# Low half of k stored in both halves of the partitions: the second score product on 128 rows

## The chip, the cores and the metric

The kernel runs on one NeuronCore of a Trainium2 chip. The metric is the device time of one execution in microseconds (us); less is better. PE is the matrix engine, PEld its weight loads, DVE, ACT and POOL the vector, scalar and GpSimd engines, SP the engine whose queue issues most DMAs.

## The reference

One decoder layer in float32 on 1024 tokens of width 1024: LayerNorm, a projection, two attention groups side by side, an output projection, LayerNorm, a SwiGLU feed-forward block (width 2816), LayerNorm. The scores of both groups are what the change touches:

```python
# stick-breaking group: 8 heads of 64, causal
z = einsum('bhqd,bkhd->bhqk', q_blk, k) * Dh ** -0.5
log_1m_beta = where(causal, log_sigmoid(-z), 0.0)
suffix = cumsum(log_1m_beta, reverse=True) - log_1m_beta
attn = where(causal, exp(log_sigmoid(z) + suffix), 0.0)
out = einsum('bhqk,bkhd->bqhd', attn, v)
# sliding-window group: 8 query heads over 2 k/v heads, window 128
logits = einsum('bnqhgd,bnchd->bnhgqc', qb, kb) * Dh ** -0.5
p = softmax(where(valid, logits + bias, -inf), with a sink logit per head)
```

## The kernel before, in words

Every float32 operand of a product is split into a high part (rounded to float32r) and a low part (the rest), and a product of two operands is made of three matrix products, high by high, high by low and low by high (`mm3`, lines 114 to 120). In the scores a head has only 64 dimensions, so the split is laid along the 128 partitions instead. The tile `q` of a head holds the high part of q on 64 partitions and the low part on the other 64 (`put_q`, L279 and L280). The tile `kd[e]` of head e holds the high part of k twice, on both halves (`put_k`, ACT, L272 and L273), so one product over 128 rows gives (q high + q low) by k high. The low part of k stands once, in one tile `kl` for two heads, head e on its own 64 partitions (`put_k`, DVE, L274). The second product of the scores reads only these 64 rows:

```python
pe.matmul(ps, qs[:, tok], kd[:, keys], start=True, stop=False)
pe.matmul(ps, qs[r, tok], kl[r, keys], start=False, stop=True)
```

These are L384 and L385 in the stick-breaking group (`sb_unit`, output `z`) and L318 and L319 in the sliding-window group (`swa_attend`, output `lg`). There are 96 and 64 such pairs.

The program runs in stages. First entry LayerNorm, with k, v and q of the first sliding-window group and its attention (to about 132 us). Then the attention of the second sliding-window group beside the projection of the first pair of stick-breaking heads (132 to 208 us). Then, for pairs 0 to 2, the attention of a pair beside the projection of the next (208 to 412 us). Then the attention of pair 3 beside the first half of the output projection (`c1_steps`, 412 to 510 us). Then the second half of the output projection and the feed-forward block, in which none of this occurs. `merge` traces two such streams side by side; a scheduler then sets the order of the instructions on every engine.

Weights come as strips of 512 KB over SP (`w_raw`, L136) into two `raw` buffers, are split by ACT (L72) and POOL (L73), and are read by the projection `pp` (L120). The tiles q, kd, kl and v, the loads `m` and `res` of the output projection, and some others share one pool of 17 buffers of 4 KB a partition (`U`, tag `u`). A pair of heads takes seven of them: two q, two kd, one kl, two v. `out_load` (L456) fetches `m`, `wo_fill` fetches `w_out` through `raw`, both over SP. SP takes its DMAs in order; one that waits holds up those behind it.

Of the kernel before, what the change touches and what calls it, by code (L numbers as in the profile page):

```python
# [16 lines left out]
ALU = mybir.AluOpType  # L17
# [4 lines left out]
P = 128  # L22
S = 1024
# [22 lines left out]
def _f(ap):  # L46
    return ap.bitcast(F32)
# [3 lines left out]
def layer(ctx: ExitStack, tc: tile.TileContext, x, ln_in, w_sw, w_sb, norm_g,  # L51
# [68 lines left out]
                pe.matmul(ps, a, b, start=(i == 0), stop=(i == n - 1))  # L120
                i += 1

    # the tokens' chunks 2 and 3 make room for the residual, 0 and 1 for half of w_out
    rp = ctx.enter_context(tc.tile_pool(name="rp", bufs=4, side="right", reuse_waits="tile"))
    c1 = ExitStack()
    c1p = c1.enter_context(tc.tile_pool(name="c1p", bufs=4, side="right", reuse_waits="tile"))
# [34 lines left out]
            yield v  # L161

    def merge(a, ta, b, tb):
        # two streams traced side by side in step with their shares; the first goes ahead
        a = ahead(a)
        ca = cb = 0.0
        while a is not None or b is not None:
            if b is None or (a is not None and ca / ta <= cb / tb):
                v = next(a, None)
                if v is None:  # L170
                    a = None
                else:
                    ca += v
            else:
                v = next(b, None)
                if v is None:
                    b = None
                else:
                    cb += v
# [7 lines left out]
    def U(shape, name, dt=F32R):  # L187
        return ub.tile(shape, dt, tag="u", name=name)
# [1 line left out]
    def attile(shape, name, dt=F32R):  # L190
        return bb.tile(shape, dt, tag="at", bufs=AB, name=name)

    # ---- entry LayerNorm
    xts = {}

    def load_x(t):
# [1 line left out]
        for h in ((slice(0, 512), slice(512, D)) if t == 0 else (slice(0, D),)):  # L198
            sp.dma_start(xts[t][:, h], x[t * P:(t + 1) * P, h])

    # the bias reaches all partitions over a product with a row of ones
    row = U([1, D], "row", F32)
    sp.dma_start(row, ln_in[1].unsqueeze(0))
    load_x(0)
# [61 lines left out]
        return ps.rearrange("p a b -> p (a b)"), slice(c0 * 256, (c0 + nc_) * 256)  # L266

    def put_k(ps, tok, kd, kl):
        # the high halves stand twice, so that one product meets both halves of q
        for e in range(2):  # L270
            a, b = slice(e * 64, e * 64 + 64), slice(64 - e * 64, 128 - e * 64)
            act.copy(kd[e][a, tok], ps[a])  # L272
            act.copy(kd[e][b, tok], ps[a])  # L273
            dve.tensor_tensor(out=kl[a, tok], in0=ps[a], in1=_f(kd[e][a, tok]), op=ALU.subtract)  # L274

    def put_q(ps, tok, q, e, hi_row):
        r = slice(e * 64, e * 64 + 64)
# [2 lines left out]
        dve.tensor_tensor(out=q[l, tok], in0=ps[r], in1=_f(q[h, tok]), op=ALU.subtract)  # L280

    def put_v(ps, c0, nc_, vts):
        # vts[e][:, t] holds [high | low] of head e for token tile t
        n = 2 * nc_
        vr = ws.tile([P, n, P], F32, tag="raw", bufs=2, name="vr")
        dve.tensor_copy(vr.rearrange("p a b -> p (a b)"), ps)
        pv = bps.tile([P, n, 2, 64], F32, tag="pp", name="pv")
        for i in range(n):
            pe.transpose(pv[:, i], vr[:, i, :], ident)
        for e in range(2):  # L290
            split_ps(pv[:, :, e, :], vts[e][:, 2 * c0:2 * c0 + n, 0, :], vts[e][:, 2 * c0:2 * c0 + n, 1, :])

    # ---- sliding-window group
    def swa_q(g, i, q, c0, nc_):
        ps, tok = xmul(strip(2 + 2 * g + i), c0, nc_)
        for e in range(2):
# [6 lines left out]
                yield 1.0  # L303

    def swa_attend(g, q, kd, kl, vts, bias):
        h = slice(g * 64, g * 64 + 64)
        for n in range(NT):
            tok = slice(n * P, (n + 1) * P)
            nk = P if n == 0 else 2 * P
            kb = nk // P  # L310
            keys = slice((n + 1) * P - nk, (n + 1) * P)
            Ls = []
            nm = st.tile([P, 4], F32, tag="nm", name="nm")
            for i in range(2):
                ps = bps.tile([P, 2, nk], F32, tag="z", bufs=ZB, name="lg")
                for e in range(2):
                    j = 2 * i + e
                    pe.matmul(ps[:, e, :], q[j][:, tok], kd[g][:, keys], start=True, stop=False)  # L318
                    pe.matmul(ps[:, e, :], q[j][h, tok], kl[h, keys], start=False, stop=True)  # L319
                L = bb.tile([P, 2, nk], F32, tag=("s1", "s2")[i], bufs=SB, name="L")  # L320
                dve.scalar_tensor_tensor(out=L, in0=ps, scalar=SCALE,
                                         in1=bias[:, 2 * i:2 * i + 2, 0:nk][:, :, ::-1],
                                         op0=ALU.mult, op1=ALU.add)
                dve.tensor_reduce(out=nm[:, 2 * i:2 * i + 2], in_=L, axis=AX.X, op=ALU.max, negate=True)
                Ls.append(L)
            hs = slice(4 * g, 4 * g + 4)
            dve.tensor_tensor(out=nm, in0=nm, in1=nsink[:, hs], op=ALU.min)
            es = st.tile([P, 4], F32, tag="es", name="es")
            dve.tensor_tensor(out=es, in0=sink[:, hs], in1=nm, op=ALU.add)
            den = st.tile([P, 4], F32, tag="den", name="den")  # L330
            for j in range(4):
                act.activation(Ls[j // 2][:, j % 2, :], Ls[j // 2][:, j % 2, :], AF.Exp, bias=nm[:, j:j + 1],
                               accum_out=den[:, j:j + 1])
            act.activation(es, es, AF.Exp)
            dve.tensor_tensor(out=den, in0=den, in1=es, op=ALU.add)
            rd = st.tile([P, 4], F32, tag="rd", name="rd")
            dve.reciprocal(rd, den)
            for i in range(2):
                pool.tensor_tensor(out=Ls[i], in0=Ls[i],
                                   in1=rd[:, 2 * i:2 * i + 2].unsqueeze(2).broadcast_to([P, 2, nk]), op=ALU.mult)  # L340
            av = bps.tile([P, 4, P], F32, tag="av", name="av")
            for b in range(kb):
                at = attile([P, 2, 4, P], "at")
                ah, al = at[:, 0], at[:, 1]
                ps = bps.tile([P, 4, P], F32, tag="tr", name="trp")
                for j in range(4):
                    pe.transpose(ps[:, j, :], Ls[j // 2][:, j % 2, b * P:(b + 1) * P], ident)
                split_ps(ps, ah, al)
                v = vts[g][:, n - kb + 1 + b].rearrange("p a d -> p (a d)")
                pe.matmul(av, v, ah, start=(b == 0), stop=False)  # L350
                pe.matmul(av, v, al, start=False, stop=(b == kb - 1))
            oT = bb.tile([P, 2, P], F32, tag="oT", name="oT")
            for e in range(2):
                r = slice(e * 64, e * 64 + 64)
                act.copy(oT[r], av[64:128, e::2, :])
                dve.tensor_tensor(out=oT[r], in0=av[0:64, e::2, :], in1=oT[r], op=ALU.add)
            for i in range(2):
                act.dma_start(o_dram[4 + 2 * g + i][:, tok], oT[:, i, :])
            yield 1.0

    # ---- stick-breaking group, two heads at a time
    def sb_project(p, qs, kd, kl, vts):
        for w in range(3):
            for c in range(2):
# [8 lines left out]
                yield 1.0  # L373

    def sb_unit(qs, kd, kl, e, qb, t0, t1, carry):
        # weights of the keys of tiles t0..t1 for one query block, walked from the right
        w = (t1 - t0) * P
        keys = slice(t0 * P, t1 * P)
        tok = slice(qb * P, (qb + 1) * P)
        s1 = bb.tile([P, w], F32, tag="s1", bufs=SB, name="s1")  # L380
        s2 = bb.tile([P, w + 1], F32, tag="s2", bufs=SB, name="s2")
        r = slice(e * 64, e * 64 + 64)
        ps = bps.tile([P, w], F32, tag="z", bufs=ZB, name="z")
        pe.matmul(ps, qs[:, tok], kd[:, keys], start=True, stop=False)  # L384
        pe.matmul(ps, qs[r, tok], kl[r, keys], start=False, stop=True)  # L385
        act.activation(s2[:, 0:w], ps, AF.Sigmoid, scale=-SCALE)
        act.activation(s1, ps, AF.Sigmoid, scale=SCALE)
        last = t1 - 1 == qb
        if last:
            # keys at or after the query neither take weight nor break the stick  # L390
            pool.affine_select(out=s1[:, w - P:], in_=s1[:, w - P:], pattern=[[-1, P]], base=0,
                               channel_multiplier=1, compare_op=ALU.is_gt, fill=0.0)
        else:
            pool.tensor_copy(s2[:, w:w + 1], carry)
# [10 lines left out]
    def sb_attend(p, qs, kd, kl, vts):  # L405
        for c in range(4):
            oT = bb.tile([P, 256], F32, tag="oT", name="oT")
            for e in range(2):
# [3 lines left out]
                for t0, t1 in ([(0, nb)] if nb <= 4 else [(4, nb), (0, 4)]):  # L412
                    ats = [attile([P, 2, 2, 2, P], "at") for u in range(t0, t1, 2)]
                    for i in range(2):
                        qb = 2 * c + i
                        te = min(t1, qb + 1)
                        A, carry[i] = sb_unit(qs[e], kd[e], kl, e, qb, t0, te, carry[i])
                        m = te - t0
                        ps = bps.tile([P, m, P], F32, tag="tr", name="tra")
                        for j in range(m):  # L420
# [19 lines left out]
                            act.dma_start(o_dram[p][:, c * 256:(c + 1) * 256], oT)  # L440
                    yield float(m)

    # ---- output projection
    def wo_fill(k, hi, lo):
        raw = w_raw(w_out[k * P:(k + 1) * P, :], (P, D))
        act.activation(hi, raw, AF.Copy, scale=gT[:, k:k + 1])
# [37 lines left out]
    def units():  # L484
        bias0 = load_bias(0)
        q0 = [U([P, S], "q") for _ in range(4)]
        kd = [U([P, S], "kd") for _ in range(2)]
        kl = U([P, S], "kl")
        vts = [U([P, NT, 2, 64], "v") for _ in range(2)]
        return bias0, q0, kd, kl, vts  # L490

# [26 lines left out]
    merge(att0, 2, swa_project(1, q1), 4)  # L518

    def sb_tiles():  # L520
        return ([U([P, S], "q") for _ in range(2)], [U([P, S], "kd") for _ in range(2)], U([P, S], "kl"),
                [U([P, NT, 2, 64], "v") for _ in range(2)])

    cur = sb_tiles()
# [54 lines left out]
                    pe.transpose(ps[:, i, :], acc[t][:, k * P:(k + 1) * P], ident)  # L579
                split_ps(ps, hh[cc][:, 4 * g:4 * g + 4, o:o + P], hl[cc][:, 4 * g:4 * g + 4, o:o + P])  # L580

    # ---- FFN and last post-LayerNorm
    fq = [(f, j) for f in range(NF) for j in range(2)]
    fl = []

# [137 lines left out]
```

## Time and profile before

| what | value |
|---|---|
| three runs | 1319.35, 1320.6, 1322.6 us, median 1320.6 |
| profiled execution, first to last instruction | 1319.7 us |
| what lies around it | no own time is listed for the profiled execution; its span stands 0.9 us under the median of the runs |
| PE busy | 1273.9 us (97%) |
| PEld, DVE, POOL, ACT busy | 1051.3, 644.3, 484.7, 472.2 us |
| mean granted PE clock | 0.987 of full speed |

Matrix products are pipelined: the next one starts before the one before it has ended. So what a product takes of PE's time is read from the start of one row of the timeline to the start of the next, not from its duration.

### The profile page before, as it was taken

Reading aid. Unit: us, or ns where it says so; the run is one execution under the profiler, and the core shown is the slowest. Engines: PE = TensorE matmul, PEld = TensorE weight load, DVE = VectorE, ACT = ScalarE, POOL = GpSimd, SP = SyncE. Lnnn points to the kernel's source line nnn. Section 1 sums busy time; section 2 is a strip of 40 time slices with the busy share of each in tenths; the row PEclk is TensorE's granted clock in tenths of the full one; section 3 lists DMA queues with packets and bytes.
Section 4 is the critical chain, followed back from the end, with each engine's and each line's share of the span. In section 5 each row is a group of like instructions: output and inputs, shape, how many; then the busy total and the mean of one; then the engine's idle time right before and its main releaser. Section 6 shows DMA issues by size and latency. Waiting matters only on the chain. (4 is left out here: it accounts for less than half of the span.)

```text
span 1319.7 us, 17018 instructions
## 1 busy us (share of the span) xinstructions
PE 1273.9 (97%) x6606; PEld 1051.3 (80%) x6606; DVE 644.3 (49%) x1028; ACT 472.2 (36%) x986; POOL 484.7 (37%) x452
## 2 busy tenths in 40 slices
PE   5799999999999999999999999999999999999997
PEld 3688988888887777878888888888888888888886
DVE  8875676787778887862242222221222123212248
ACT  4565566766667654442032002200221022102111
POOL 5413333555545856763042004210321032103224
PEclk9899999999999899999999999999999999999999
DMA  7212102010104411112122102200221022102112
GB/s 268 85 40 73 33 13 60 17 53 13 54 20 137 135 56 59 46 65 80 32 80 64 32 16 80 65 32 16 67 77 32 16 64 80 32 16 64 33 51 109
DMA packets 31919, 78.25 MB, mean 59 GB/s; under 512 B 3764, under 2 KB 15069, under 8 KB 31838
## 3 DMA queue, kind: packets, MB, share of 16 engines
q1 hardware_dynamic: 23614, 68.49, 16.3%
q10 hardware_dynamic: 8224, 8.67, 1.9%
q8 instruction: 52, 0.85, 0.3%
q14 instruction: 29, 0.24, 0.1%
HBM read 64.55 MB, written 12.60 MB: 58 GB/s over the span
## 5 line engine op out<-in xcount | busy, mean ns | idle before, releaser
L73 POOL TENSOR_TENSOR wlo<-raw,whi 128x1024 fp32r<-128x1024 f32 x61 | 146.3, 2400 | 390.2 <-ACT whi L72 387.0
L120 PE MATMUL pgu<-hl,whi 128*128 128x512 f32 x704 | 277.5, 394 | 0.0
L120 PE MATMUL pgu<-hh,wlo 128*128 128x512 f32 x704 | 277.5, 395 | 0.0
L120 PE MATMUL pgu<-hh,whi 128*128 128x512 f32 x704 | 277.3, 394 | 0.0
L627 DVE SCALAR_TENSOR_TENSOR acc<-acc,pd 128x512 f32<-128x512 f32 (+1 forms) x97 | 65.9, 681 | 215.2 <-PE pd L120 215.2
L120 PE MATMUL pp<-xh,whi 128*128 128x256 f32 x544 | 160.1, 295 | 0.4 <-DVE q L280 0.4
L120 PE MATMUL pp<-xh,wlo 128*128 128x256 f32 x544 | 157.7, 290 | 0.0
L609 DVE TENSOR_TENSOR sg<-sg,pgu 128x512 f32<-128x512 f32 x44 | 30.2, 687 | 261.2 <-PE pgu L120 260.8
L120 PEld LDWEIGHTS pgu<-hh,wlo 128*128 128x128 f32 x704 | 131.8, 187 | 32.2
L120 PEld LDWEIGHTS pgu<-hl,whi 128*128 128x128 f32 x704 | 131.8, 187 | 32.1
L120 PEld LDWEIGHTS pgu<-hh,whi 128*128 128x128 f32 x704 | 131.7, 187 | 32.2 <-ACT sg L606 0.2
L120 PE MATMUL pp<-xl,whi 128*128 128x256 f32 x544 | 156.8, 288 | 0.0
L72 ACT CAST whi<-raw 128x1024 fp32r<-128x1024 f32 x61 | 64.1, 1051 | 258.4 <-PE pgu L120 204.7
L120 PE MATMUL pd<-wdl,ah 128*128 128x512 f32 (+1 forms) x356 | 138.1, 388 | 0.0
L120 PE MATMUL pd<-wdh,ah 128*128 128x512 f32 (+1 forms) x356 | 137.8, 387 | 0.0
L120 PE MATMUL pd<-wdh,al 128*128 128x512 f32 (+1 forms) x356 | 137.7, 387 | 0.0
L120 PEld LDWEIGHTS pp<-xh,whi 128*128 128x128 f32 x544 | 105.1, 193 | 5.1 <-issue 2.3
L120 PEld LDWEIGHTS pp<-xh,wlo 128*128 128x128 f32 x544 | 104.6, 192 | 4.3 <-issue 2.9
L120 PEld LDWEIGHTS pp<-xl,whi 128*128 128x128 f32 x544 | 105.1, 193 | 3.6 <-issue 2.4
L73 POOL TENSOR_TENSOR wdl<-raw,wdh 128x1024 fp32r<-128x1024 f32 x22 | 54.8, 2495 | 135.8 <-ACT wdh L72 135.8
L399 POOL TENSOR_TENSOR s<-s,s 128x127 f32<-128x127 f32 (+2 forms) x96 | 86.6, 905 | 45.8 <-DVE s L395 20.7
L612 DVE TENSOR_TENSOR al<-sg,ah 128x512 fp32r<-128x512 f32 x44 | 78.3, 1781 | 46.9 <-ACT ah L611 46.9
(146 smaller groups left out, 2178.6 us busy)
## 6 DMA issues: line engine op xcount, KB each, us to landing
raw<-in_w_gu SPq DMA_DIRECT2D x44, 512.0 KB, 3.6
raw<-in_w_down SPq DMA_DIRECT2D x22, 512.0 KB, 3.6
raw<-in_w_sb SPq DMA_DIRECT2D x12, 512.0 KB, 3.7
h_dram<-x ACTq DMA_DIRECT2D x8, 512.0 KB, 2.9
m<-o_dram SPq DMA_DIRECT2D x32, 128.0 KB, 2.5
res<-h_dram SPq DMA_DIRECT2D x8, 512.0 KB, 3.9
raw<-in_w_out SPq DMA_DIRECT2D x8, 512.0 KB, 4.2
x<-in_x SPq DMA_DIRECT2D x7, 512.0 KB, 6.8
```

What stands on the lines that cost most here:

```text
L72: act.copy(hi, raw)
L73: pool.tensor_tensor(out=lo, in0=raw, in1=_f(hi), op=ALU.subtract)
L120: pe.matmul(ps, a, b, start=(i == 0), stop=(i == n - 1))
L399: pool.tensor_tensor(out=s1[:, 0:m], in0=s1[:, 0:m], in1=s2[:, 1:m + 1], op=ALU.mult)
L609: dve.tensor_tensor(out=sg, in0=sg, in1=ps, op=ALU.mult)
L612: dve.tensor_tensor(out=al[:, tok], in0=sg, in1=_f(ah[:, tok]), op=ALU.subtract)
L627: dve.scalar_tensor_tensor(out=acc[t][:, ds], in0=acc[t][:, ds], scalar=(ALPHA if ci == 0 else 1.0), in1=pd, op0=ALU.mult, op1=ALU.add)
```

## The change

`kl` becomes a list of two tiles, one a head, as `kd` is. DVE writes the low part of k on the head's own 64 partitions as before, and a DMA on SP's queue copies it to the other 64 partitions of the same tile. Both second products then read all 128 rows: q high and q low, each by k low. The low by low term, which the kernel before left out, is so added to the scores. A pair takes eight buffers of the pool of 17.

```diff
 def put_k(ps, tok, kd, kl):
     for e in range(2):
         a, b = slice(e * 64, e * 64 + 64), slice(64 - e * 64, 128 - e * 64)
         act.copy(kd[e][a, tok], ps[a])
         act.copy(kd[e][b, tok], ps[a])
-        dve.tensor_tensor(out=kl[a, tok], in0=ps[a], in1=_f(kd[e][a, tok]), op=ALU.subtract)
+        dve.tensor_tensor(out=kl[e][a, tok], in0=ps[a], in1=_f(kd[e][a, tok]), op=ALU.subtract)
+        sp.dma_start(_f(kl[e][b, tok]), _f(kl[e][a, tok]))
...
 def swa_attend(g, q, kd, kl, vts, bias):
-    h = slice(g * 64, g * 64 + 64)
...
                 pe.matmul(ps[:, e, :], q[j][:, tok], kd[g][:, keys], start=True, stop=False)
-                pe.matmul(ps[:, e, :], q[j][h, tok], kl[h, keys], start=False, stop=True)
+                pe.matmul(ps[:, e, :], q[j][:, tok], kl[g][:, keys], start=False, stop=True)
...
 def sb_unit(qs, kd, kl, e, qb, t0, t1, carry):
-    r = slice(e * 64, e * 64 + 64)
     pe.matmul(ps, qs[:, tok], kd[:, keys], start=True, stop=False)
-    pe.matmul(ps, qs[r, tok], kl[r, keys], start=False, stop=True)
+    pe.matmul(ps, qs[:, tok], kl[:, keys], start=False, stop=True)
...
-                        A, carry[i] = sb_unit(qs[e], kd[e], kl, e, qb, t0, te, carry[i])
+                        A, carry[i] = sb_unit(qs[e], kd[e], kl[e], e, qb, t0, te, carry[i])
...
-        kl = U([P, S], "kl")
+        kl = [U([P, S], "kl") for _ in range(2)]
```

`sb_tiles` allocates `kl` in the same way. The rest of the diff takes comments away.

The copies take places in SP's queue. Before, from the load of the second window group's bias to the first `m` (`w_sw` and `w_sb` are the strips of the two groups; the last two rows are the first two of eight loads of `m`):

```order
L243 DMA bias<-e_dram 128x4x256
L136 DMA raw<-in_w_sw 128x1024
L136 DMA raw<-in_w_sb 128x1024 x12
L456 DMA m<-o_dram_84 128x256
L456 DMA m<-o_dram_85 128x256
```

In the change, from the strip ahead of that bias on:

```order
L136 DMA raw<-in_w_sw 128x1024
L275 DMA kl<-kl 64x256 x2
L243 DMA bias<-e_dram 128x4x256
L275 DMA kl<-kl 64x256 x6
L136 DMA raw<-in_w_sw 128x1024
L136 DMA raw<-in_w_sb 128x1024 x4
L275 DMA kl<-kl 64x512 x4
L136 DMA raw<-in_w_sb 128x1024 x3
```

Eight copies for the window groups and four for each of the four pairs stand between the strips. After the rows shown come four copies, three strips, four copies, two strips and four copies; then the eight loads of `m`, which the copies of pair 3 now precede.

Behind these `m` the order on SP before was this (`res` is the residual, `w_out` the output projection's weight):

```order
L545 DMA res<-h_dram_73 128x1024
L456 DMA m<-o_dram_84 128x256
L456 DMA m<-o_dram_85 128x256
L456 DMA m<-o_dram_86 128x256
L136 DMA raw<-in_w_out 128x1024
L456 DMA m<-o_dram_87 128x256
```

In the change:

```order
L545 DMA res<-h_dram_73 128x1024
L136 DMA raw<-in_w_out 128x1024
L455 DMA m<-o_dram_84 128x256
L455 DMA m<-o_dram_85 128x256
L455 DMA m<-o_dram_86 128x256
L455 DMA m<-o_dram_87 128x256
L136 DMA raw<-in_w_out 128x1024
```

The first load of `w_out` moves up past three loads of `m`, to right behind the residual.

On PE the order is that of before, but for one exchange of a few rows in the window groups, until the first product of the output projection (`pr`, then `pc`) beside the attention of pair 3. Before:

```order
L384 MATMUL z<-kd,q 128x256
L385 MATMUL z<-kl,q 128x256
L433 MATMUL av<-at,v 128x256
L432 MATMUL av<-at,v 128x256
L433 MATMUL av<-at,v 128x256
L432 MATMUL av<-at,v 128x256
L470 MATMUL pr<-ones,m 128x1
L120 MATMUL pc<-wo_5230,whi 128x512 x2
```

In the change:

```order
L432 MATMUL av<-at,v 128x256
L431 MATMUL av<-at,v 128x256
L432 MATMUL av<-at,v 128x256
L469 MATMUL pr<-ones,m 128x1
L120 MATMUL pc<-wo_5259,whi 128x512 x2
L120 MATMUL pc<-wo_5259,wlo 128x512
L120 MATMUL pc<-wo_5260,whi 128x512
L431 MATMUL av<-at,v 128x256
L383 MATMUL z<-kd,q 128x256
L384 MATMUL z<-kl,q 128x256
```

The output projection begins eight to eleven products earlier, ahead of a pair of scores that it followed. From there to the end of the attention the two streams are shuffled differently.

## Rows read from the trace of the kernel before

**Rows 1.** The page's first line: the span.

```profile
span 1319.7 us, 17018 instructions
```

**Rows 2.** Windows, one a stage: length, busy us of each engine (instructions), PE's granted clock, DMA share, GB/s.

```profile
50.00:132.00 82.00, 76.70 (x499) 66.75 (x500) 52.16 (x115) 45.53 (x130) 21.66 (x18) 0.94 0.19 65
132.00:208.00 76.00, 76.00 (x526) 66.54 (x527) 51.17 (x111) 44.26 (x124) 22.54 (x19) 1.00 0.07 20
208.00:412.00 204.00, 203.09 (x1456) 176.46 (x1454) 153.96 (x256) 140.60 (x344) 106.27 (x169) 1.00 0.14 41
412.00:446.00 34.00, 29.68 (x155) 23.71 (x154) 31.72 (x41) 24.54 (x53) 29.59 (x29) 0.80 0.50 165
446.00:510.00 64.00, 63.30 (x310) 47.98 (x309) 49.93 (x74) 35.65 (x77) 43.51 (x59) 1.00 0.25 81
```

**Rows 3.** Who PE waited for, 208 to 412 us: total, times, longest.

```profile
PE av L433 <- DVE at L77: 0.3, 1, 0.3
```

**Rows 4.** The same view, 50 to 132 us.

```profile
PE trx L255 <- DVE xl L77: 4.3, 1, 4.3
PE pp L120 <- DVE v L77: 2.4, 1, 2.4
```

**Rows 5.** Timeline of PE, pairs 0 and 1: start, duration, line, product, rows*columns, times.

```profile
300.86 0.28 PE L120 MATMUL pp<-xh,whi 128*128 128x256 f32 x1
300.97 0.40 PE L384 MATMUL z<-kd,q 128*128 128x512 f32 x1
301.30 0.50 PE L385 MATMUL z<-kl,q 64*128 64x512 f32 x1
301.72 0.38 PE L120 MATMUL pp<-xl,whi 128*128 128x256 f32 x1
...
310.93 0.28 PE L384 MATMUL z<-kd,q 128*128 128x256 f32 x1
311.14 0.38 PE L385 MATMUL z<-kl,q 64*128 64x256 f32 x1
311.45 0.66 PE L421 MATMUL tra<-ident,s 128*128 128x128 f32 x4
```

**Rows 6.** Timeline of the weight loads, the same place; in brackets idle time before.

```profile
300.86 0.19 PEld L384 LDWEIGHTS z<-kd,q 128*128 128x128 f32 x1
301.29 0.18 PEld L385 LDWEIGHTS z<-kl,q 64*128 64x128 f32 x1 [0.25 <-issue]
301.72 0.19 PEld L120 LDWEIGHTS pp<-xl,whi 128*128 128x128 f32 x1 [0.24 <-issue]
```

**Rows 7.** Timeline of PE in the feed-forward block: 512 columns on 128 rows.

```profile
899.90 0.39 PE L120 MATMUL pd<-wdh,al 128*128 128x512 f32 x1
900.13 0.40 PE L120 MATMUL pd<-wdh,ah 128*128 128x512 f32 x1
900.36 0.39 PE L120 MATMUL pd<-wdl,ah 128*128 128x512 f32 x1
```

**Rows 8.** Windows with the products of L319 alone: PE, PEld, clock, DMA share, GB/s.

```profile
50.00:132.00 82.00, 11.96 (x32) 5.85 (x32) 0.94 0.19 65
132.00:208.00 76.00, 11.95 (x32) 5.85 (x32) 1.00 0.07 20
```

**Rows 9.** Windows with the products of L385 alone.

```profile
208.00:412.00 204.00, 29.32 (x69) 12.25 (x69) 1.00 0.14 41
412.00:446.00 34.00, 4.25 (x9) 1.92 (x9) 0.80 0.50 165
446.00:510.00 64.00, 8.09 (x18) 3.29 (x18) 1.00 0.25 81
```

**Rows 10.** DMA issues: queue, times, KB each, median us to landing.

```profile
m<-o_dram SPq DMA_DIRECT2D x32, 128.0 KB, 2.5
```

**Rows 11.** Timelines of DVE and SP: pair 1's last `kl`, and the strips behind it.

```profile
266.10 0.69 DVE L274 TENSOR_TENSOR kl<-pp,kd 64x512 fp32r<-64x512 f32 x1 [0.71 <-ACT kd L273]
...
274.11 17.49 SPq L136 DMA_DIRECT2D raw<-in_w_sb  x3
```

**Rows 12.** Timeline of SP: first eight `m` and first `w_out`.

```profile
356.19 44.89 SPq L456 DMA_DIRECT2D m<-o_dram  x8
...
412.27 0.33 SPq L136 DMA_DIRECT2D raw<-in_w_out  x1
```

More of the change, by code (lines that the diff above doesn't have):

```diff
@@ L520, in sb_tiles @@
     def sb_tiles():
-        return ([U([P, S], "q") for _ in range(2)], [U([P, S], "kd") for _ in range(2)], U([P, S], "kl"),
+        return ([U([P, S], "q") for _ in range(2)], [U([P, S], "kd") for _ in range(2)],
+                [U([P, S], "kl") for _ in range(2)],
                 [U([P, NT, 2, 64], "v") for _ in range(2)])
```

## The prediction
> **What bounds the kernel now.** I read the busy times by stage first, then PE's own waits, then the timeline of PE around a pair of score products, and last SP's queue. The span is 1319.7 us [rows 1], 0.9 us under the median of the three runs. The windows [rows 2] show where the changed products lie. From 132 to 412 us PE is busy all the time (279 of 280 us) at full clock, while DVE, the next engine, is busy for 51 of 76 us and then 154 of 204 us. The waits say the same: from 208 to 412 us PE was held up by another engine four times, never for longer than 0.3 us [rows 3]. So in these stages whatever PE no longer spends is time gained, until another engine comes up to it. From 446 to 510 us PE is again busy for 63.3 of 64 us. Two stretches are different. From 50 to 132 us PE is busy for 76.7 of 82 us and waits for DVE, 4.3 us at the longest [rows 4]. From 412 to 446 us, where pair 3 starts and the output projection is not yet fed, PE is busy for 29.7 of 34 us at a mean clock of 0.80, and DVE is the full engine, at 31.7 of 34.
>
> Busy time does not tell what a product costs, since products overlap. In the timeline [rows 5] I take start to start. A product of 256 columns on 128 rows takes 0.11 us (300.86 to 300.97). One of 512 columns takes 0.23 us where full products follow each other [rows 7]. But the first product of a score pair, 512 columns, takes 0.33 us until the 64-row product starts, and that one 0.42 us until the next full product starts. The weight loads show why [rows 6]: the load for L385 and the one after it each stand behind an idle stretch of about 0.25 us that ends in "issue", while the load for L384, between full products, has none. The change of the number of rows, into 64 and out of it again, holds the next load back until the running product is almost through. The load itself is not what differs: 0.18 us against 0.19.
>
> **The change, part by part.** *Second products on 128 rows.* With 512 columns the pair takes 0.33 + 0.42 = 0.75 us and would take 2 x 0.23 = 0.46, so 0.29 less. With 256 columns [rows 5] it takes 0.21 + 0.31 = 0.52 us and would take 2 x 0.11 = 0.22 to 0.23, again 0.29 less. I take 0.29 us for every pair, whatever its width. The count by stage [rows 8, 9]: 32 pairs from 50 to 132 us, 32 from 132 to 208, 69 from 208 to 412, 9 from 412 to 446, 18 from 446 to 510, 160 in all, or 46.4 us of PE time.
>
> How much of this reaches the end:
> - 132 to 208, 208 to 412 and 446 to 510 us hold 119 pairs, 34.5 us. PE is the bound there, so the upper end is all of it. After the gain the long stage lasts 204 - 20 = 184 us, and DVE's 154 us fill 84% of it instead of 75%. No row shows PE full beside a DVE at 84%; at 75% PE loses nothing, and at 93% (412 to 446 us) it loses 4.3 of 34 us, partly because no projection is there to fill in. For the lower end I let 84% cost what 93% does, an eighth of the remaining 310 us, which would leave nothing of the gain; that is too dark, as DVE's work there holds no weight fill, and half of it leaves some 15 us. I take nine tenths, since 84 still lies on the side where every other engine has a sixth of its time free: 31 us.
> - 50 to 132 us hold 9.3 us. PE waits there for the entry LayerNorm, and faster scores don't bring that forward. Bounds 0 and 9.3; since PE is busy for 94% of it, I take 6 us.
> - 412 to 446 us hold 2.6 us. DVE is the bound, so 0, with 2.6 as the other end.
>
> *DVE's subtraction* writes as many elements as before, to another tile: nothing. *The low by low term* costs no product of its own, it rides in the rows that were empty.
>
> *24 copies on SP.* They move 64 or 128 KB. The nearest row is the 128 KB load of `m`, 2.5 us to landing [rows 10]; a copy within the chip's own memory isn't in the trace. Against the gain I allow from 1 to 5 us each. They are covered: pair 1's last `kl` is written at 266.8 us and the next strip is issued at 274.1 [rows 11], so four copies, one behind the other at the 2.5 us of that row, would hold SP's queue for 10 us at the worst, some 3 us past the place of the strip, and at their issue alone for far less. I take pairs 0 and 2 to be alike. If that cover were gone, a late strip would stop PE for the few us that are missing, three times, some 9 us. Cost taken: 0.
>
> *One buffer more a pair.* Two pairs hold 16 of 17 buffers instead of 14. So only one `m` can be loaded before pair 2 has been read to its end, where before the first eight loads of `m` went out from 356 to 401 us [rows 12]. The second `m` and the residual now wait for tiles of pair 2, and the first `w_out` stands behind them in SP's queue. That load goes out at 412.3 us today, close to the end of pair 2, so I take 0; the bad end is the third rival.
>
> The sum: 31 + 6 = 37 us. 1319.7 - 37 = 1282.7 us for the span, 1283.6 on the scale of the median; I say **1283 us**.
>
> **The rivals.** *The 64 rows are not the cause.* The extra time could come from the second product following the first on the same output and the same q. Then it stays with 128 rows and the time is 1320.6, with the copies hidden. Against it: the three products of a projection follow each other on one output just so, at 0.11 us each, and the stretch that ends in "issue" also stands before the load that comes *after* the 64-row product, which belongs to another output. A rule of the Trainium skill speaks for this rival: "TensorE: Matmul & The Clock Gate", in the section "Why this matters for your kernels", says that a single product on 32 rows takes the time of one on 128, so widening would buy nothing. The trace agrees as to the load (0.18 against 0.19 us) and not as to the step from start to start (0.42 against 0.23). Chance 0.05.
>
> *Another engine takes over.* DVE, or the chain from scores over sigmoid, scan and transposition back to PE, sets the pace once PE is some 10% faster. Half of the gain or less is left, 10 to 30 us: 1300 as its middle. For it: DVE is full in 412 to 446 us, and PE lost time there. Against it: every engine but PE has a quarter or more of its time free in the long stage. Chance 0.17.
>
> *Slower: the output projection starves.* The place is SP's queue at pair 3. If the second `m` waits for the last tile of pair 2 rather than an early one, the first `w_out` comes later than 412.3 us, by 10 us as an estimate, and the three behind it, each needing a buffer that the former holds, could lose as much again: up to 40 us, as then PE runs pair 3 alone and the projection after it. It decides once the delay is over 37 us: 1323 us. Against it: half of pair 2's tiles belong to its first head and come free before its end. Chance 0.04.
>
> *All of it is gained.* PE stays the bound in every stretch: 46.4 us, 1274. For it: the waits of rows 3 are next to nothing. Chance 0.12.
>
> **How the numbers follow.** The forecast, a gain of 30 to 42 us, has 0.62. The range, 1273 to 1300 us, holds it, the case in which all is gained, and the better half of the case in which another engine takes over; what is left out is the worse half of that one (0.085), the two rivals without a gain (0.09) and a little beyond 1273. A measurement of this kernel can tell 0.3%, 4 us, from no change. Faster by more: 0.62 + 0.17 + 0.12 = 0.91. Within 0.3%: 0.05. Slower: 0.04.
>
> **What would show it.** In the timeline of the changed kernel a score pair of 512 columns should take 0.46 us from start to start of the next product, one of 256 columns 0.23, and the loads should have no stretch of 0.25 us ending in "issue". The stage of pairs 0 to 2 should last about 186 us instead of 204, with PE still full and its waits for DVE and ACT at a few us. The copies should land before the products that read them, with none of those products waiting for a DMA. From the first `w_out` on, the start of pair 3 should look as it does now. I am wrong if pairs still take 0.75 us (the rows are not the cause), if PE shows gaps behind DVE or ACT in the long stage that add up to over 10 us, or if strips or `w_out` are issued later against the stage that they feed.

## The result and the profile after

The median on record of the changed kernel is 1278.9 us, that of the kernel before 1320.3 us (1319.4 to 1322.6), 41.4 us apart. Three executions of the changed kernel took 1277.2, 1278.2 and 1279.5 us; the fourth, the profiled one, took 6249.7 us with every matrix product several times slower, counts in that median and says nothing of the change. Without it the ratio is 0.9675 with a 95% interval of 0.966 to 0.9691, some 43 us less. In the experiments below the change was run twice more beside the kernel before, with 0.9677 (0.9661 to 0.9693) and 0.9688 (0.9675 to 0.9701). The rows after are from the first of these, `e1_after`.

From the page after, the span and the busy us of each engine (share of the span, instructions):

```profile
span 1277.1 us, 17071 instructions
PE 1224.2 (96%) x6606; PEld 1045.3 (82%) x6606; DVE 645.1 (51%) x1028; ACT 468.2 (37%) x986; POOL 491.0 (38%) x452
```

PE carries out as many products as before (6606), and its busy time falls by 1273.9 - 1224.2 = 49.7 us. Its idle time grows from 45.8 to 52.9 us, so 42.6 us of the span are left as the gain. DVE, ACT and POOL carry out as many instructions as before; their busy times change by 0.8, -4.0 and 6.3 us.

The timeline of PE after, at pairs of 512 and 256 columns, against [rows 5]:

```profile
277.97 0.28 PE L120 MATMUL pp<-xh,whi 128*128 128x256 f32 x1
278.09 0.39 PE L383 MATMUL z<-kd,q 128*128 128x512 f32 x1
278.32 0.40 PE L384 MATMUL z<-kl,q 128*128 128x512 f32 x1
278.55 0.28 PE L120 MATMUL pp<-xl,whi 128*128 128x256 f32 x1
278.67 0.28 PE L431 MATMUL av<-at,v 128*128 128x256 f32 x1
...
286.56 0.28 PE L383 MATMUL z<-kd,q 128*128 128x256 f32 x1
286.68 0.28 PE L384 MATMUL z<-kl,q 128*128 128x256 f32 x1
286.80 0.60 PE L420 MATMUL tra<-ident,s 128*128 128x128 f32 x4
```

From start to start the pair of 512 columns takes 278.55 - 278.09 = 0.46 us instead of 0.75, the pair of 256 columns 0.24 instead of 0.52.

That is not yet the whole difference. In the kernel before, the full product behind the pair was slow as well. The row that follows on those of [rows 5] is this:

```profile
301.94 0.28 PE L432 MATMUL av<-at,v 128*128 128x256 f32 x1
```

From its start at 301.72 to this row the full product of 256 columns took 0.22 us, after the change 0.12 (278.55 to 278.67). PE's order is the same in both places, and over pair and next product the difference is 0.97 - 0.58 = 0.39 us, not 0.29. The traces hold 86 such places in which PE's order is the same in both kernels and no other 64-row product stands near; their middle values are 0.28 us up to the next full product and 0.39 up to the one behind it, and nothing is added further on.

The weight loads of the same place, against [rows 6]:

```profile
277.98 0.19 PEld L383 LDWEIGHTS z<-kd,q 128*128 128x128 f32 x1
278.09 0.19 PEld L384 LDWEIGHTS z<-kl,q 128*128 128x128 f32 x1
278.32 0.19 PEld L120 LDWEIGHTS pp<-xl,whi 128*128 128x128 f32 x1
```

Neither the load of the second product nor the one behind it has an idle stretch before it any more. Each starts as soon as the product before it has started, so it lies wholly beside running work.

The windows from the first of the second products (z from `kl`) of one stick-breaking pair of heads to the first of the next, pairs 0 to 2, and then pair 3 to its last; before (length, busy us of PE, PEld, DVE, ACT and POOL, clock, DMA share, GB/s):

```profile
211.20:285.70 74.50, 73.59 (x524) 63.44 (x522) 56.12 (x94) 53.15 (x128) 39.09 (x61) 1.00 0.13 41
285.70:354.80 69.10, 69.10 (x499) 60.14 (x497) 53.16 (x86) 46.64 (x115) 38.01 (x59) 1.00 0.11 32
354.80:425.10 70.30, 69.80 (x502) 60.73 (x501) 54.08 (x87) 48.52 (x119) 36.05 (x58) 1.00 0.22 71
425.10:509.60 84.50, 79.98 (x373) 60.66 (x372) 68.82 (x98) 50.41 (x109) 64.01 (x76) 0.92 0.32 103
```

After:

```profile
191.50:262.70 71.20, 67.81 (x525) 63.46 (x524) 56.62 (x94) 52.67 (x128) 40.92 (x62) 1.00 0.18 51
262.70:324.60 61.90, 60.80 (x498) 59.13 (x498) 52.08 (x85) 45.34 (x115) 38.47 (x58) 1.00 0.15 44
324.60:388.40 63.80, 61.32 (x503) 59.73 (x502) 54.78 (x90) 48.05 (x120) 39.60 (x59) 1.00 0.24 75
388.40:472.90 84.50, 77.37 (x406) 64.64 (x405) 73.82 (x104) 50.99 (x112) 67.79 (x79) 0.94 0.37 119
```

Each stage holds 24 pairs of score products, 24 x 0.39 = 9.4 us (in the stage of pair 0 they stand in 22 stretches, 8.6 us). Pairs 1 and 2 give 7.2 and 6.5 us, pair 0 only 3.3. The beginning, up to the first second product of pair 0, is shorter by 211.2 - 191.5 = 19.7 us. Pair 3 seems to give nothing, but its stage now carries more of the output projection (406 products instead of 373); what comes after it is shorter by 5.9 us.

Most of those 19.7 us lie in the two window groups, 32 pairs of products each. From the first second product of the first group to that of the second group, and from there to the last; before:

```profile
52.20:146.40 94.20, 90.48 (x612) 80.02 (x610) 60.33 (x134) 55.62 (x154) 25.93 (x21) 0.95 0.20 64
146.40:207.40 61.00, 61.00 (x410) 52.28 (x409) 40.72 (x88) 33.89 (x100) 16.07 (x14) 1.00 0.05 13
```

After:

```profile
51.00:138.50 87.50, 81.91 (x612) 78.86 (x612) 60.27 (x134) 54.88 (x153) 25.53 (x21) 0.91 0.23 73
138.50:188.00 49.50, 49.50 (x410) 48.55 (x410) 39.93 (x86) 33.47 (x99) 16.09 (x14) 1.00 0.11 28
```

The second group is the cleanest place of the two traces: PE is full, at 2.4 GHz and without a wait before and after, and carries out the same 410 products. It gives 11.5 us, 0.36 us a pair. That is a little less than 0.39, which fits nine places of the kernel before where a single full product stands between two 64-row ones and nothing is left to be late behind it. The first group gives 6.7 us.

PE's waits in the stages of pairs 0 to 2, against [rows 3]. First the whole answer from 191 to 262.5 us:

```profile
PE av L432 <- DVE at L77: 1.7, 3, 0.8
PE tra L420 <- DVE at L77: 0.8, 3, 0.5
PE av L350 <- ACT at L76: 0.5, 1, 0.5
PE av L351 <- DVE at L77: 0.2, 1, 0.2
```

Then from 262.5 to 388 us:

```profile
PE av L432 <- DVE at L77: 2.3, 2, 1.3
PE pv L290 <- DVE vr L287: 0.7, 1, 0.7
PE tra L420 <- POOL s L390: 0.4, 1, 0.4
```

Together 6.6 us, where there were four waits of at most 0.3 us. PE now meets, here and there, results of DVE that aren't ready. In these three stages PE's busy time falls by 22.6 us (212.5 to 189.9) and its idle time grows by 5.6 (1.4 to 7.0), which leaves the 17.0 us.

### The profile page after: what moved, and what is told of

Its sections match the earlier page's. It is cut to its first block, busy times and chain, and to the rows that moved or that the text cites. A ratio compares the mean times of both kernels' runs of the same rounds, so it can differ in the third digit from the quotient of the medians.

```text
span 6248.0 us, 17071 instructions
## 1 busy us (share of the span) xinstructions
PE 6234.3 (100%) x6606; PEld 4635.5 (74%) x6606; DVE 602.7 (10%) x1028; ACT 485.3 (8%) x986; POOL 465.6 (7%) x452
## 5 line engine op out<-in xcount | busy, mean ns | idle before, releaser
L120 PE MATMUL pgu<-hl,whi 128*128 128x512 f32 x704 | 1051.7, 1494 | 0.0
L120 PE MATMUL pgu<-hh,wlo 128*128 128x512 f32 x704 | 1051.1, 1494 | 0.0
L120 PE MATMUL pgu<-hh,whi 128*128 128x512 f32 x704 | 1048.0, 1490 | 0.0
L120 PEld LDWEIGHTS pgu<-hh,wlo 128*128 128x128 f32 x704 | 530.5, 754 | 280.8 <-issue 280.8
L120 PE MATMUL pp<-xh,whi 128*128 128x256 f32 x544 | 576.0, 1060 | 0.0
L120 PE MATMUL pp<-xh,wlo 128*128 128x256 f32 x544 | 572.9, 1053 | 0.0
L120 PE MATMUL pp<-xl,whi 128*128 128x256 f32 x544 | 568.5, 1045 | 0.0
L120 PEld LDWEIGHTS pp<-xh,wlo 128*128 128x128 f32 x544 | 508.8, 935 | 14.0 <-issue 14.0
L120 PEld LDWEIGHTS pp<-xl,whi 128*128 128x128 f32 x544 | 507.8, 933 | 10.6 <-issue 10.6
L120 PEld LDWEIGHTS pp<-xh,whi 128*128 128x128 f32 x544 | 508.3, 935 | 9.8 <-issue 9.6
```

## The experiments

Each was timed beside the kernel before on the same chip, which took 1321.5 to 1322.2 us there. Two repeat the change, one leaves the rows as they were, four place the price, and three ask what takes part of the gain back. An edit is shown against the changed kernel unless the text names the kernel before; `...` marks left-out lines.

**The changed kernel once more.**

> The changed kernel as it is, for a profile to read stage by stage beside the others. If the row change of the 64-row products was the cost, a pair of score products of 512 columns takes 0.46 us from start to start of the next product instead of 0.75, one of 256 columns 0.23 instead of 0.52, the stage of pairs 0 to 2 lasts 184 to 187 us instead of 204, and the whole 1277 to 1280 us. If another engine had taken over part of the pace, PE's waits for DVE and ACT in that stage add up to 5 us or more.

Measured: 1279.0 us against 1322.0. The pairs are as expected. The three stages of pairs 0 to 2, in the windows above, last 196.9 us together instead of 213.9, 17.0 us less where 17 to 20 were expected. The waits above come to 6.6 us, over the 5 us that were named as the sign of another engine with part of the pace: PE is still the bound, though no longer everywhere.

**The copies and the buffer alone.**

```diff
-                    pe.matmul(ps[:, e, :], q[j][:, tok], kl[g][:, keys], start=False, stop=True)
+                    h = slice(g * 64, g * 64 + 64)
+                    pe.matmul(ps[:, e, :], q[j][h, tok], kl[g][h, keys], start=False, stop=True)
...
-        pe.matmul(ps, qs[:, tok], kl[:, keys], start=False, stop=True)
+        r = slice(e * 64, e * 64 + 64)
+        pe.matmul(ps, qs[r, tok], kl[r, keys], start=False, stop=True)
```

> The change without its gain: k low is stored twice, with all 24 copies and the eighth buffer of a pair, but both second products read 64 rows as before. If copies and buffer cost nothing, it takes the time of before, 1319 to 1322 us. If they cost something that the gain hid, the time is longer by that: 46.4 us of PE time were saved and 41 came out, so up to 5 us, 1325.

Measured: 1321.5 us against 1322.0, a ratio of 0.9994 (0.9985 to 1.0004). So the 24 copies and the eighth buffer cost nothing that can be measured. They do move work: here the last second product of the scores starts at 515.9 us instead of 509.6, yet the first product of the feed-forward block (`pgu`) starts at 566.5 instead of 565.1. The scheduler deals out more of the output projection beside pair 3 (404 products in that stage instead of 373) and leaves less for later. Measured against this kernel, pair 3 too gains in the change: its stage lasts 90.1 us here (425.8 to 515.9) and 84.5 in the change, with 404 and 406 products.

**Both products on 64 rows, in the kernel before.** The product of q low by k high is left out.

```diff
-                    pe.matmul(ps[:, e, :], q[j][:, tok], kd[g][:, keys], start=True, stop=False)
+                    pe.matmul(ps[:, e, :], q[j][h, tok], kd[g][h, keys], start=True, stop=False)
...
-        pe.matmul(ps, qs[:, tok], kd[:, keys], start=True, stop=False)
+        pe.matmul(ps, qs[r, tok], kd[r, keys], start=True, stop=False)
```

> The kernel before with both products of the scores on 64 rows (q low by k high is left out), 320 products on 64 rows instead of 160. If the price lies in the change of the number of rows, a pair pays it once as before: 1310 to 1322 us, with the window groups' pairs, which follow each other in twos, a little cheaper. If a product on 64 rows is slow by itself, it pays twice: 1355 to 1367 us.

Measured: 1321.2 us, a ratio of 0.9995 (0.9984 to 1.0005), with 320 products on 64 rows instead of 160, in 150 stretches (64-row products with no full one between them) instead of 158. A product on 64 rows is not slow by itself: at a price a product the expectation had 33 us more at the least. That it came out the same to a microsecond is chance: in the trace the window groups are 9.2 us shorter (146.0 instead of 155.2, in 53 stretches instead of 64) and the rest of the program is longer by about as much. The timeline shows where the price went (pairs of 512 columns first, then two pairs of 256 columns in a row):

```profile
293.67 0.28 PE L120 MATMUL pp<-xh,whi 128*128 128x256 f32 x1
293.88 0.49 PE L384 MATMUL z<-kd,q 64*128 64x512 f32 x1
294.21 0.39 PE L385 MATMUL z<-kl,q 64*128 64x512 f32 x1
294.53 0.39 PE L120 MATMUL pp<-xl,whi 128*128 128x256 f32 x1
...
174.48 0.28 PE L120 MATMUL pp<-xl,whi 128*128 128x256 f32 x1
174.69 0.38 PE L318 MATMUL lg<-kd,q 64*128 64x256 f32 x1
174.91 0.28 PE L319 MATMUL lg<-kl,q 64*128 64x256 f32 x1
175.03 0.28 PE L318 MATMUL lg<-kd,q 64*128 64x256 f32 x1
175.15 0.28 PE L319 MATMUL lg<-kl,q 64*128 64x256 f32 x1
175.35 0.39 PE L120 MATMUL pp<-xh,wlo 128*128 128x256 f32 x1
175.58 0.29 PE L120 MATMUL pp<-xh,whi 128*128 128x256 f32 x1
```

With two 64-row products the way from the full product before to the full one after is 294.53 - 293.67 = 0.86 us; full products would take 0.115 + 0.23 + 0.23 = 0.575, so 0.285 more. With four it is 175.35 - 174.48 = 0.87 against 5 x 0.115 = 0.575, 0.295 more. Behind the four, the full product too takes 0.23 us (175.35 to 175.58) instead of 0.115. Up to the next full product a stretch of 64-row products costs 0.29 us, whether one [rows 5], two or four stand in it, and the delay of that product comes on top.

**The stick-breaking group alone, and the window groups alone.** In each, the other group keeps one `kl`, no copies and 64 rows (`put_k` copies only where told):

```diff
+    def put_k(ps, tok, kd, kl, twice=True):
...
+            if twice:
+                sp.dma_start(_f(kl[e][b, tok]), _f(kl[e][a, tok]))
```

> The change in the stick-breaking group alone, 96 of the 160 pairs; the window groups keep one k low and 64 rows. With 0.29 us a pair the 87 pairs in the stages in which PE is the bound give 25 us, 1295 us. The other 64 pairs are then worth the rest of the gain, 16 us, if the stage up to 132 us passes most of it on, and 9 to 10 us if it keeps it for itself; in that case this run stands at 1288.

> The change in the window groups alone, 64 of the 160 pairs; the stick-breaking group keeps one k low and 64 rows. The stick-breaking pairs alone gave 22.7 us of the 43. If the two add up, this one gives 20 us, 1302; 64 x 0.29 = 18.6 would be 1303.5. If the stage up to 132 us kept part of it for itself, 1306 or more.

Measured: 1299.3 us against 1322.0 for the stick-breaking group (0.9832, 0.9817 to 0.9847), 22.7 us less; 1302.6 us against 1322.2 for the window groups (0.9854, 0.984 to 0.9867), 19.6 us less. The two add up to 42.3 of 43. At 0.36 to 0.39 us a stretch the 64 of the window groups hold 23 to 25 us and pass on 19.6, the 94 of the stick-breaking group hold 34 to 37 us and pass on 22.7. The first expectation named 1295 us, or 1288 if the early stage kept its part; 1299 is outside, since the stick-breaking stages gave less than I had taken: those of pairs 0 to 2 last 197.9 us here instead of 213.9, 16.0 us less.

**Two 64-row products side by side, in the kernel before.**

```diff
-                    pe.matmul(ps[:, e, :], q[j][:, tok], kd[g][:, keys], start=True, stop=False)
-                    pe.matmul(ps[:, e, :], q[j][h, tok], kl[h, keys], start=False, stop=True)
+                    two = [(q[j][:, tok], kd[g][:, keys]), (q[j][h, tok], kl[h, keys])]
+                    for n_, (qa, ka) in enumerate(two if e == 0 else two[::-1]):
+                        pe.matmul(ps[:, e, :], qa, ka, start=(n_ == 0), stop=(n_ == 1))
```

> The kernel before, with the two products of every second head of a window group in the other order (k low first), so that two 64-row products can follow each other. In the order of its instructions 160 products on 64 rows then stand in 139 stretches instead of 158. If 0.29 us is the price of a stretch, 19 x 0.29 = 5.5 us less than before, 1315 to 1318. If it is the price of a product, nothing: 1320 to 1323.

Measured: 1316.4 us against 1322.2, a ratio of 0.9948 (0.9936 to 0.9961), 6.9 us less by the ratio (5.2 to 8.5; 5.8 between the medians) where 5.5 were expected; 19 stretches at 0.36 to 0.39 us would be 6.8 to 7.4. The trace has 139 stretches instead of 158, and it is shorter where the order was changed: the window groups last 147.0 us instead of 155.2. Nothing was widened here and no byte is moved, only the order of products. This tells the price of a stretch from the price of a product most directly. One such place:

```profile
175.00 0.28 PE L320 MATMUL lg<-kd,q 128*128 128x256 f32 x1
175.22 0.50 PE L320 MATMUL lg<-kl,q 64*128 64x256 f32 x2
175.65 0.39 PE L320 MATMUL lg<-kd,q 128*128 128x256 f32 x1
175.87 0.28 PE L120 MATMUL pp<-xh,wlo 128*128 128x256 f32 x1
```

The two 64-row products take 0.43 us until the next full one, where one took 0.31 [rows 5]: the second costs 0.12 us, what a full product of its width takes. The full one behind them takes 0.22 us here too (175.65 to 175.87).

**The copies on DVE instead of the DMA.**

```diff
-            sp.dma_start(_f(kl[e][b, tok]), _f(kl[e][a, tok]))
+            dve.tensor_tensor(out=kl[e][b, tok], in0=ps[a], in1=_f(kd[e][b, tok]), op=ALU.subtract)
```

> The change with its 24 copies made by DVE (a second subtraction in put_k, on the other 64 partitions) instead of the DMA: 24 subtractions more, 16 of 0.68 and 8 of 0.41 us, 14 us of DVE. If DVE now sets part of the pace beside the attention of a pair, where it is busy for 80 to 86% of the time, the stages of pairs 0 to 2 grow by about the 2.7 us of DVE that each gets, and the whole by 5 to 14 us, 1284 to 1293. If PE's own work is still the whole bound, it stays at 1277 to 1281.

Measured: 1283.0 us (0.9702, 0.9688 to 0.9715). That lies below the range I had named for a DVE that sets the pace and above the one for a DVE that doesn't. The change itself had 0.9677 and 0.9688, and the intervals overlap, so a loss against it is not shown. The 24 subtractions take 14 us; DVE's busy time as a whole is 9.8 us up (654.9 against 645.1). In the two profiled executions, 4.2 us apart, 3.0 us lie in the stages of pairs 0 and 1 (136.1 us instead of 133.1, with 1036 products instead of 1023). There PE waited 1.7 us for ACT at one place where it waited 0.5 in the change, and from 200.8 to 207.4 us, just behind it, its granted clock was 0.50, the lower level of 1.2 GHz, where the change has 1.00. Those 6.6 us at half speed can cost up to 3.3 us. So the run doesn't show that DVE sets the pace; most of the 14 us is hidden.

**Work taken from DVE.** First all of `put_v`'s copy out of the accumulator:

```diff
-        dve.tensor_copy(vr.rearrange("p a b -> p (a b)"), ps)
+        act.copy(vr.rearrange("p a b -> p (a b)"), ps)
```

> The change with the copy of v out of the accumulator (put_v) on ACT instead of DVE: 1.4 us of DVE less in each of the four stick-breaking stages, a little more on ACT. If PE's 3 to 4 us of waits for DVE beside the attention of each pair are DVE being too full, the whole comes out 1 to 4 us shorter, 1275 to 1278. If they are the latency of one chain, or if ACT's delay takes it back, it stays at 1277 to 1281 or grows.

Measured: 1282.6 us (0.9699, 0.9686 to 0.9712), some 3 us above the change by the medians, with intervals that overlap. The stages of pairs 0 to 2 are about as long as in the change (196.1 us against 196.9). From pair 3 to the end it takes 897.2 us instead of 888.7, as the scheduler ordered the output projection and the feed-forward block differently (373 products in pair 3's stage instead of 406). So the whole time doesn't answer the question. The next one keeps PE's order at that place, with ACT taking the copy for half of the tokens:

```diff
-        dve.tensor_copy(vr.rearrange("p a b -> p (a b)"), ps)
+        (act.copy if nc_ == 1 or c0 == 0 else dve.tensor_copy)(vr.rearrange("p a b -> p (a b)"), ps)
```

> The change with the copy of v on ACT for the first half of the tokens of each pair and for the first window group, on DVE for the rest. With the whole copy on ACT the scheduler had dealt the output projection out differently and the end of the program lost what the attention might have won; here the first and last products of that stage stand at the same places of PE's order as in the change. If PE's waits for DVE and ACT in the attention stages are DVE being too full, 1 to 3 us less than the change in the same comparison, 1276 to 1278. If they are one chain's latency, no difference, 1278 to 1280.

> The change once more, on the same chip as the run beside it, for the difference of the two: 1278 to 1280 us.

Measured on one chip: 1277.9 us (0.967, 0.9657 to 0.9683) against 1279.7 us for the change (0.9688, 0.9675 to 0.9701). It is lower by 1.8 us, but the intervals overlap, so it is no shown gain. Nor does it lie where the question was asked. In the profiled executions the stages of pairs 0 to 2 last 199.0 us against 197.2 for the change; what is shorter is the time before them (187.4 us against 192.1). In the window groups PE's mean granted clock is 0.98 in this run (51.6 to 187.4 us) and 0.95 in the change (53.0 to 192.1 us), so this run stood at the lower level of 1.2 GHz for less of the time.

## Why the prediction was right, and where its sum was off

The forecast was 1283 us in a range of 1273 to 1300; measured are 1278.9. The direction, the cause and the range hold. That the number came out so near is in part luck: the price of a pair was taken too small, and the share of it that reaches the end too large.

- *The price, 0.29 us a pair.* That the price lies in going to 64 rows and back is right, and shown three ways: the pairs after (0.46 and 0.24 us), the run with 320 products on 64 rows and no rise in time, and the run in which putting them side by side saved 6.9 us. Its size is too small. The working ends at the start of the next full product, and that product was slow too (301.72 to 301.94 us, 0.22 us instead of 0.115). The price is 0.39 us where a pair stands alone, and 0.36 a pair over the second window group. The prediction counted 160; as two 64-row products twice followed each other directly, there are 158 stretches, so 57 to 62 us instead of 46.4. Of these, 1322.0 x (1 - 0.9677) = 42.7 us came out.
- *119 pairs in the stages bound by PE, nine tenths, 31 us.* The second window group (32 pairs, 8.4 us in that sum) gave 11.5 us: there all of it came through. The long stage (69 pairs, 18.0 us) gave 17.0 in the windows of pairs 0 to 2, not nine tenths but some two thirds of the 25 to 27 us that their 70 stretches hold. Pair 3 with what follows it takes 84.5 + (565.1 - 509.6) us before and 84.5 + (523.1 - 472.9) after, 5.3 us of 9. In pairs 0 to 2, 5.6 us of what is missing are new idle time of PE; the rest is not placed.
- *50 to 132 us, 6 of 9.3 us.* The first window group gave 94.2 - 87.5 = 6.7 us, about the number that was forecast, though at 0.36 to 0.39 us its 32 pairs hold 11.5 to 12.5. PE's waits in that window grow from 3.7 to 5.6 us, 3.4 of them for v from DVE, and its mean granted clock falls from 0.95 to 0.91, with more of the time at the lower level of 1.2 GHz. By an estimate from these two rows, the clock alone takes 0.09 x 87.5 - 0.05 x 94.2 = 3.2 us back. The sum had the waits in view, the clock not.
- *412 to 446 us, 0 of 2.6 us.* Can't be told apart: the output projection is dealt out differently there.
- *The copies, 0.* Right. They land in 2.2 us (128 KB) and 1.9 us (64 KB), within the 1 to 5 us that I allowed and close to the row I went by [rows 10], and the run with them alone took 0.9994 of the time before. SP's queue after, at pair 3, against [rows 12]:

```profile
355.90 13.84 SPq L275 DMA_DIRECT2D kl<-kl  x4
369.84 6.14 SPq L455 DMA_DIRECT2D m<-o_dram  x8
376.08 0.85 SPq L545 DMA_DIRECT2D res<-h_dram  x2
377.09 0.33 SPq L136 DMA_DIRECT2D raw<-in_w_out  x1
```

  The eight `m` follow the copies at once, and the first `w_out` is issued 388.4 - 377.1 = 11.3 us before pair 3's scores begin, where it was 425.1 - 412.3 = 12.8 us. So the slower rival, a starving output projection, didn't come about. Two readings on the way to this term were off, without harm: two `m` tiles (eight loads) and two residuals went out before pair 2 had ended, where the prediction had room for one `m`; and four copies held SP's queue for 10.9 to 13.8 us, where it had 10 as the worst. No wait of PE in these stages names a DMA. The copies' landing times are these:

```profile
kl<-kl SPq DMA_DIRECT2D x16, 128.0 KB, 2.2
kl<-kl SPq DMA_DIRECT2D x8, 64.0 KB, 1.9
```
- *The rows are not the cause* fell with the pairs' own time: the second product still follows the first on the same output and the same q, and the extra time is gone. The statement of the Trainium skill, "TensorE: Matmul & The Clock Gate", section "Why this matters for your kernels", that a single product on 32 rows takes the time of one on 128 is not contradicted for the product itself: on 64 rows, inside a stretch, one of 256 columns takes 0.12 us (174.91 to 175.03), as a full one does; none on 32 rows was run. What entering and leaving such a stretch costs is not in that statement. Another page of the Trainium skill, "TensorEngine Tiling (Array Packing)", section "Key Properties", says that a change of the tiling mode drains the engine; the rows fit that, with 0.36 to 0.39 us for the way in and out, but no run here shows that this is what happens.
- *Another engine takes over* came true in part. PE's waits in the stages of pairs 0 to 2 went from 0.9 to 6.6 us. Whether DVE's load (80 to 86% there) or the latency of the chain through it makes these waits stays open: neither the 14 us laid on DVE nor the copies of v taken from it changed the time by more than the intervals allow, and with half of the copies taken away these stages did not get shorter.

## What to carry to other kernels

Read PE's cost from start to start, not from busy time: the weight load that couldn't start early shows as a step that is 0.1 to 0.2 us longer and an "issue" stretch, and no wait of any engine names it. Read on behind the place until the steps are the usual ones again; here the working ended one product too early and missed a quarter of the price. Where PE is the bound and single products with fewer rows stand between full ones, fill the empty rows (here with a copy that a DMA makes off the path) or at least put such products side by side; the price belongs to the stretch, 0.36 to 0.39 us here, not to the product. A stage in which PE is full, without waits and at one clock before and after, tells the price best. When a forecast comes out, compare it term by term before trusting its parts.

## What the runs showed of the hardware that I had not expected

The price of leaving and entering is spread differently by what stands in the stretch: one 64-row product starts some 0.1 us late and the full one behind it another 0.19; with two it is 0.1, 0.1 and 0.09. Where that full one has 256 or 512 columns, the product behind it starts some 0.11 us late too (middle values 0.223 and 0.338 us instead of 0.115 and 0.23). The width of the 64-row product makes no difference: the middle values of its step to the next full one are 0.253, 0.311 and 0.425 us at 128, 256 and 512 columns, each 0.19 to 0.2 more than a full product of that width takes (0.06, 0.115 and 0.23). In the kernel before, two 64-row products for the two heads of a pair, on different halves of the rows, twice followed each other directly. They ran beside each other, the one of 256 and the one of 384 columns starting 3 ns apart (the first row merges them):

```profile
223.86 0.44 PE L385 MATMUL z<-kl,q 64*128 64x256 f32 x2
224.23 0.39 PE L120 MATMUL pp<-xh,wlo 128*128 128x256 f32 x1
```

The next full product starts 0.37 us later, as it does behind a single one of 384 columns (middle value 0.366). If all of them were paired so, two of 512 columns would take some 0.1 us for the way in, 0.42 until the next full product and 0.11 behind it, 0.63 us against 0.46 for two full ones: an estimate from these rows of 0.17 us more than the change for two pairs, without copies. It was not tried.
